# A hybrid encoder block on one Trainium2 core: the residual stream laid out features by tokens from the output projection on, with the second norm's token scale on gate and gated tiles

## The chip, the cores and the metric

The kernel runs on one core of a Trainium2 chip. The metric is the device time of one execution in microseconds. Engines are named as in the profile: PE is TensorE (matmuls), PEld its weight loads, DVE VectorE, ACT ScalarE, POOL GpSimd, SP SyncE, which issues most DMAs.

## What is computed

One layer over 1024 tokens and 1024 features, in fp32:

```
h = rms_norm(x, norm1_g);  z = h @ w_in
conv_out = conformer_conv(a, gate of z);  attn_out = neighbourhood_attention(q, k, v of z)
x = x + concat(conv_out, attn_out) @ w_out
h = rms_norm(x, norm2_g)          # x / sqrt(mean(x*x over features) + eps) * norm2_g
x = x + (silu(h @ w_gate) * (h @ w_up)) @ w_down      # 2816 hidden features
```

The norm's token scale r = 1/sqrt(...) is one number a token. Since h = (x * norm2_g) * r, gate and up products of x * norm2_g can be multiplied by r afterwards, token by token, as long as r is applied before silu.

## The kernel before

**Matmuls.** Every matmul of the projections is made of three: `mac` (L122, L123, L124) multiplies hi x hi, hi x lo and lo x hi parts. `split` (L113 to L118) makes the parts: ScalarE casts the hi part (L114), VectorE or GpSimd subtracts it from the source for the lo part (L118). The stationary operand is 128 x 128, the moving one 128 x 512. The three big products (output projection, gate and up, down projection) each use a scheme of seven products instead of eight, with sums and differences of quadrants. The quadrants are halves of the tokens (x11, x12 first half, x21, x22 second) by halves of the features.

**Order.** It is written out by hand. `weaves(n, s0=..., s1=...)` makes a list of n entries; after each mac of a product, `weave()` runs the next entry. So `s9=N(0)` puts `norm2_out(0)` behind the tenth mac. `plan[k]` is such a list of four for the k-th product of the FFN. The scheduler places instructions on each engine's queue in program order; an engine runs its queue in order and waits at the head for its operands.

**Output projection** (`group` L1112, `proj` L770, `read` L874). Seven products in the order n1, n7, n4, n6, n5, n2, n3; each has four output tiles of four macs, that is 48 matmuls. The left operand's token tile (128 tokens, from attention output `a11`, or convolution and sums in `qop`) is stationary, 512 features of the weights `wB` or `wP` move, and an output tile holds 128 tokens x 512 features. `fill` runs the first tile of n1 in the last steps of attention. Each result is added on VectorE (L865) into `x2[t]`, one tile of 128 tokens x 1024 features for each of eight t, into which the block's input x is loaded or accumulated by DMA.

**Second norm.** Behind n5 and n3, `norm2(t)` (L943) stores x2[t] to DRAM, squares it on ScalarE with a sum over the row, and takes the root. `norm2_out(t)` (L954) makes xn = x2 * r * g on VectorE. Then `turn(t, j)` (L1067), 16 times, transposes four 128 x 128 blocks of xn on TensorE, since the next products contract over features; ScalarE and VectorE take them out of PSUM: for the first token half straight into hi and lo parts `h2` (the operands A11 and A12), and into `xT`. `s_sum` (L1037, and L1033 for S4, part of it on GpSimd) makes the sums S1 to S4, and `s_split` (L118) their parts and those of A22, all by tiles of 128 tokens.

**Gate and up** (`product` L1166, `evac` L1177). The weight parts `t` are stationary, the token operands move, and results are 128 hidden features x 512 tokens. There are 22 blocks i, each with seven products. The first four are run interleaved in this order, and these are the numbers that `plan` and the prediction use: 0 to 7 are m1(0), m1(1), m2(0), m2(1), m1(2), m1(3), m2(2), m2(3); 8 to 17 are m6(0), m6(1), m5(0), m5(1), m7(0), m7(1), m3(0), m3(1), m4(0), m4(1). m6 reads S2, m5 S1, m7 S3, m3 S4, m4 A22. A product is four macs, 12 matmuls. After each, `prep` splits one more weight tile, the lo part on GpSimd. `evac` combines results: u = B - g (L1185), g = B - g (L1193), g = g - D (L1195), g = B - g (L1197), D = D - u (L1201), the silu on ScalarE (L1191, L1202), and silu x up (L1198, L1205). From block 4 on all seven products of one block follow each other (the FFN's steady part).

**Down projection** (`down` L1358). Seven products over `sd`, which comes back from DRAM; again 128 tokens are stationary and 512 features move.

Of the kernel before, what the change touches and what calls it, by code (L numbers as in the profile page):

```python
# [13 lines left out]
P = 128  # L14
# [17 lines left out]
def layout(v):  # L32
# [21 lines left out]
        "x": f["x"],  # L54
        "xt": f["x"].T.reshape(4, 2, P, 2, 512).transpose(3, 0, 2, 1, 4),
# [6 lines left out]
        "g2": f["norm2_g"][None],  # L62
# [12 lines left out]
def build(ctx, tc, a):  # L75
# [622 lines left out]
    def evac_hi(s_):  # L698
        rh, cb = order[s_]
        if rh == 0:  # L700
            if not rowf:
                rowf.extend(G(f"rf{j}").rearrange("p (c b q) -> p c b q", c=2, b=4) for j in range(2))
            for j in range(2):
                act.copy(rowf[j][:, :, cb], os_[s_][:, 2 * j:2 * j + 2])
        else:
            a11[cb] = [w.rearrange("p (c q) -> p c q", c=4) for w in lr(G(f"a11{cb}", F32R))]
            act.copy(a11[cb][0], os_[s_])

    def evac_lo(s_, js=(0, 1)):
        rh, cb = order[s_]  # L710
        if rh == 0:
            return
        if not diff:
            diff.extend(G(f"df{j}").rearrange("p (c b q) -> p c b q", c=2, b=4) for j in range(2))
        for j in js:
            cs = slice(2 * j, 2 * j + 2)
            hi, lo = [w[:, cs] for w in a11[cb]]
            dve.tensor_tensor(lo, os_[s_][:, cs], hi.bitcast(F32), OP.subtract)
            dve.tensor_tensor(diff[j][:, :, cb], os_[s_][:, cs], rowf[j][:, :, cb], OP.subtract)
# [38 lines left out]
    x2, xn, qop = {}, {}, {}  # L758
# [9 lines left out]
    CB = (0, 3, 1, 2)  # L768
# [83 lines left out]
    def rows(ap, t):  # L852
        rh, cb = divmod(t, 4)
        return ap.rearrange("(h i w) d -> h i w d", h=2, w=GW)[rh, :, cb * 16:cb * 16 + 16, :]

    def load_x2(t):
        x2[t] = G(f"x2{t}")
        nc.sync.dma_start(x2[t], rows(a["x"], t))

    def add_x(t):  # L860
        return lambda: pool.dma_start(x2[t], rows(a["x"], t), accum_op=OP.add)
# [7 lines left out]
    def fill(*cs):  # L869
        if 0 not in pb:  # L870
            pb[0] = mm("n10")
        proj("n1", 0, pb[0], cs)

    def read(p, cb):  # L874
        acc = pb[cb]
        if p == "n1":
            x2[4 + cb] = G(f"x2{4 + cb}")
            l, r = lr(x2[4 + cb])
            act.copy(l, acc)
            dve.tensor_scalar(r, acc, -1.0, None, op0=OP.mult)  # L880
        elif p == "n7":
            put(cb, 1, acc, OP.subtract)
            put(cb, 0, acc)
        elif p in ("n4", "n6"):
            put(cb, 0, acc, OP.add if p == "n4" else OP.subtract)
        elif p == "n5":
            put(cb, 1, acc)
            put(4 + cb, 1, acc)
            norm2(cb)
        elif p == "n2":  # L890
            put(4 + cb, 0, acc)
        else:
            put(4 + cb, 1, acc)
            norm2(4 + cb)
# [3 lines left out]
    for i in range(2, 32 + 2):  # L898
# [32 lines left out]
        if i > 2:  # L931
# [3 lines left out]
            elif i > 6 and i % 4 in (0, 3):  # L935
                evac_lo((i + 1) // 4 - 2, (0,) if i % 4 == 3 else (1,))
        if jobs:
# [3 lines left out]
    sd2 = {}  # L941
# [8 lines left out]
    def norm2_out(t):  # L950
        r = SM(f"r2{t}r", 1)
        dve.reciprocal(r, sd2[t])
        xn[t] = G(f"xn{t}")
        dve.scalar_tensor_tensor(xn[t], x2[t], r, g2b, OP.mult, OP.mult)  # L954
# [66 lines left out]
    sn, sop, xT = {}, {}, {}  # L1021

    def s_sum(t, ns, eng):
        (x11, x12), (x21, x22) = lr(xT[t]), lr(xT[t + 4])
        for n in ns:
            if n == 1:
                sn[t] = G(f"sn{t}")
            s1, s2 = lr(sn[t])
            if n == 4:
                if not s4:  # L1030
                    s4.extend(G(f"s4{j}").rearrange("p (k s) -> p k s", s=512) for j in range(2))
                for j in range(2):
                    eng.tensor_tensor(s4[j][:, :, t * P:(t + 1) * P], *[w[:, j * 256:(j + 1) * 256].rearrange(  # L1033
                        "p (k s) -> p k s", s=P) for w in (x12, s2)], OP.subtract)
                continue
            o, l, r = ((s1, x21, x22), (s2, x11, s1), (x21, x11, x21))[n - 1]
            eng.tensor_tensor(o, l, r, OP.subtract)  # L1037

    s4 = []

    def s_rows(n, t):
        return {"S1": lambda: sn[t][:, :512], "S2": lambda: sn[t][:, 512:], "S3": lambda: xT[t + 4][:, :512],
                "A22": lambda: xT[t + 4][:, 512:]}[n]()

    def s_split(n, t, eng=dve):
        if n == "S4":
# [354 lines left out]
```

## Time and profile before

| | |
|---|---|
| runs (3) | 1050.26, 1050.57, 1051.03 us |
| profiled execution | 1050.14 us, of which the span from first to last instruction is 1048.4 us |
| granted TensorE clock, mean | 0.999 |
| busy: PE, PEld, DVE, ACT, POOL | 1028.2, 833.8, 722.9, 465.3, 452.6 us |
| HBM read, written | 122.86 MB, 53.15 MB |

Busy time is the union of an engine's instructions. A group row of the profile names line, engine, operation, output<-input with buffer numbers left out, shapes and count; then total busy time, the mean of one in ns, and the engine's idle time just before them. A row of the timeline is start, duration, engine, line, operation and operands. Projection, attention and convolution fill the span up to about 330 us (n1 begins among them at 317); n2 begins at 380.0 us, product 0 at 406.4.

### The profile page before, as it was taken

The numbers are of one execution on the slowest core, as the hardware profiler recorded it, in microseconds if no ns is written. First come the engines' busy times: TensorE is split into PE (matmuls) and PEld (weight loads), VectorE is DVE, ScalarE is ACT, GpSimd is POOL, SyncE is SP. The second block draws the span as 40 slices with busy tenths as digits, with TensorE's granted clock in tenths as the row PEclk, the third lists the DMA queues.
The fourth block names the chain that finished last, engine by engine and source line by source line (L and its number), as shares of the span: only waits on it lengthen the run. The fifth ranks groups of instructions, "written<-read, shape, count | busy, mean of one in ns | idle before, by whom it ended". The sixth has DMA issues, their size and how long they took to land.

```text
span 1048.4 us, 13903 instructions
## 1 busy us (share of the span) xinstructions
PE 1028.2 (98%) x4972; PEld 833.8 (80%) x4972; DVE 722.9 (69%) x1097; ACT 465.3 (44%) x915; POOL 452.6 (43%) x342
## 2 busy tenths in 40 slices
PE   7999999999999999999999999999999999999997
PEld 5888888776657888778888888888888888888885
DVE  6768998976896575876564655646556567768883
ACT  6466346636776676532232232232322443443441
POOL 0226578833575863655545454455454100002310
PEclk9999999999999999999999999999999999999999
DMA  9496771285536754465232132232232597633641
GB/s 334 178 271 220 225 238 61 77 244 168 148 109 163 159 182 141 109 167 174 104 131 101 71 131 101 89 132 93 99 111 81 207 326 256 205 101 125 215 133 40
DMA packets 74678, 162.93 MB, mean 155 GB/s; under 512 B 13489, under 2 KB 22193, under 8 KB 73905
## 3 DMA queue, kind: packets, MB, share of 16 engines
q1 hardware_dynamic: 67776, 144.14, 40.7%
q0 software_dynamic: 4864, 10.49, 5.9%
q10 hardware_dynamic: 1968, 7.42, 2.0%
q8 instruction: 39, 0.64, 0.2%
q14 instruction: 31, 0.25, 0.1%
HBM read 122.86 MB, written 53.15 MB: 168 GB/s over the span
## 4 chain that ended last, share of the span: by engine, by line
PE 88%; DVE 4%; POOL 2%; DMA 2%; ACT 2%; issue 2%; SPq 0%; POOLq 0%; ACTq 0%; DVEq 0%
PE B L122 5%; PE B L123 5%; PE B L124 5%; PE D L123 4%; PE D L124 4%; PE D L122 4%; PE A L122 3%; PE A L123 3%; PE A L124 3%; PE z L123 3%; PE z L122 3%; PE z L124 3%; PE gl L124 3%; PE gl L123 3%; PE gl L122 3%; PE n L122 3%
## 5 line engine op out<-in xcount | busy, mean ns | idle before, releaser
L347 DVE SCALAR_TENSOR_TENSOR cv<-u,par,cv 128x1009 f32<-128x1009 f32 (+14 forms) x85 | 108.5, 1276 | 2.0
L373 POOL TENSOR_TENSOR pa<-pa,pr 128x1022 f32<-128x1022 f32 (+10 forms) x31 | 75.2, 2426 | 33.7 <-ACT pr L372 32.2
L1356 POOL TENSOR_TENSOR ou<-ou,resm 128x512 f32<-128x512 f32 x8 | 12.5, 1571 | 142.5 <-DMA resm<-xd 142.5
L114 ACT CAST op<-sr 128x512 fp32r<-128x512 f32 x77 | 47.7, 619 | 52.7 <-PE B2d L124 21.3
L118 DVE TENSOR_TENSOR op<-sr,op 128x512 fp32r<-128x512 f32 x77 | 58.2, 756 | 16.4 <-ACT op L114 16.4
L1193 DVE TENSOR_TENSOR g<-B,g 128x512 f32<-128x512 f32 x22 | 15.2, 690 | 71.3 <-PE B L124 68.2
L1202 ACT ACTIVATE D<-D 128x512 f32<-128x512 f32 x22 | 12.8, 582 | 112.5 <-DVE D L1201 112.5
L1185 DVE TENSOR_TENSOR u<-B,g 128x512 f32<-128x512 f32 x22 | 15.2, 691 | 61.0 <-PE B L124 61.0
L668 POOL TENSOR_SCALAR e<-e,rs 128x288 f32<-128x288 f32 (+1 forms) x64 | 35.0, 568 | 45.6 <-DVE rs L666 41.0
L114 ACT CAST op<-wd 128x512 fp32r<-128x512 f32 x66 | 40.9, 620 | 30.4 <-DVE wd L1280 17.4
L118 DVE TENSOR_TENSOR op<-wd,op 128x512 fp32r<-128x512 f32 x66 | 50.5, 765 | 1.9 <-ACT op L114 0.3
L986 DVE TENSOR_TENSOR ts<-ts,gu 128x512 f32<-128x512 f32 x36 | 43.3, 1203 | 0.6
L1191 ACT ACTIVATE A<-A 128x512 f32<-128x512 f32 x18 | 10.5, 582 | 68.6 <-PE A L124 68.6
L661 ACT ACTIVATE e<-e,mx 128x288 f32<-128x288 f32 (+1 forms) x64 | 36.3, 569 | 2.9 <-DVE mx L659 2.8
L659 DVE CUSTOM_DVE_ANT_0 e<-s,tab 128x288 f32<-128x288 f32 (+1 forms) x64 | 29.7, 501 | 8.7 <-PE s L646 8.4
L372 ACT ACTIVATE pr<-u,par 128x1022 f32<-128x1022 f32 (+10 forms) x31 | 34.2, 1135 | 1.2 <-ACT vs L433 1.2
L677 PEld LDWEIGHTS p<-ident,e 128*96 128x96 f32 (+1 forms) x192 | 20.0, 133 | 18.1 <-POOL e L668 10.4
L677 PE MATMUL p<-ident,e 128*96 128x128 f32 (+1 forms) x192 | 28.5, 281 | 2.3 <-DVE pT L682 1.0
L986 DVE TENSOR_TENSOR ts<-gu 128x512 f32<-128x512 f32 x18 | 30.1, 1670 | 0.0
L865 DVE TENSOR_TENSOR x<-x,n 128x512 f32<-128x512 f32 x32 | 21.0, 681 | 13.1 <-PE n L124 13.1
L693 PE MATMUL o<-pT,vw 96*64 96x128 f32 (+1 forms) x384 | 28.0, 281 | 0.0
L646 PE MATMUL s<-kT,qT 64*128 64x288 f32 (+1 forms) x128 | 26.7, 495 | 0.0
(1066 smaller groups left out, 3524.1 us busy)
## 6 DMA issues: line engine op xcount, KB each, us to landing
sr<-sd SPq DMA_DIRECT2D x77, 256.0 KB
gu<-in_gu SPq DMA_DIRECT2D x36, 512.0 KB
sd<-sd SPq DMA_DIRECT2D x22, 512.0 KB
wd<-in_wd SPq DMA_DIRECT2D x44, 256.0 KB
sd<-g SPq DMA_DIRECT2D x33, 256.0 KB
x<-in_x SPq DMA_DIRECT2D x12, 512.0 KB
xd<-x SPq DMA_DIRECT2D x8, 512.0 KB
resm<-xd SPq DMA_DIRECT2D x16, 256.0 KB
```

What stands on the lines that cost most here:

```text
L114: act.copy(hi, src)
L118: eng.tensor_tensor(*[w[..., sl] for w in (lo, src, hi.bitcast(F32))], OP.subtract)
L122: pe.matmul(acc, lh, rh, start=start, stop=False, skip_group_check=True)
L123: pe.matmul(acc, lh, rl, start=False, stop=False, skip_group_check=True)
L124: pe.matmul(acc, ll, rh, start=False, stop=stop, skip_group_check=True)
L347: dve.scalar_tensor_tensor(acc[:, o], uc[:, i], dwk[:, c, t:t + 1], acc[:, o], OP.mult, OP.add)
L372: act.activation(pr[:, o], uc[:, i], AF.Copy, scale=dwk[:, c, t:t + 1])
L373: pool.tensor_tensor(pa[:, o], pa[:, o], pr[:, o], OP.add)
L661: act.activation(e[:, hh], e[:, hh], AF.Exp, bias=mx, scale=-1.0, accum_out=rs[:, hh:hh + 1])
L668: pool.tensor_scalar(es[i][:, hh], es[i][:, hh], rs[:, hh:hh + 1], 1.0, op0=OP.mult, op1=OP.mult)
L677: pe.transpose(pt[:m, g * P:(g + 1) * P], es[i][:, hh, g * m:(g + 1) * m], ident)
L986: dve.tensor_tensor(lr(tsum[i, 1])[n - 3] if o is None else o, l, r, OP.add)
```

## The change

From the output projection on, the weights are stationary and the tokens move, so that each result is 128 features x 512 tokens. Then:

- x2[t] holds, for a token half and a group jb, two tiles of 128 features x 512 tokens. The host hands over x (`x2`) in that layout and lays the output out again; `g2` comes as 128 x 8 numbers into `par`.
- The 16 turns (64 transposes), `norm2`, `norm2_out` and xn are gone. Squares are summed elementwise into one tile for each token half (ScalarE squares, VectorE adds), `token_sums` (TS) sums over the features by four F32 matmuls with a column of ones, VectorE takes the inverse root by small steps (RS; v is its input), and `token_rows` (TR) spreads it over all partitions by four transposes of a broadcast column, copied by ScalarE into `rw` (128 x 1024, a half for each token half).
- Left operands are split with the feature scale g2 in one step (`split2`: ScalarE for hi, a scalar_tensor_tensor on VectorE for lo). The sums S1 to S4 are made in place, all on VectorE, S1 with x22 scaled by ScalarE into PSUM (Y).
- The token scale `rw` is multiplied in `evac`: for the gate tile before silu and for silu x up after it (m2 and m4): four more 128 x 512 operations on VectorE a block.
- n1's first two tiles are cut, since the last window's tokens (columns 256 to 384 of 512) come late: an EARLY part of 256 and 128 columns, and a LATE part of 128.
- Window 0's attention output is parked and its parts split later (`early_split`).
- In the down projection the two operands change places.

The core of the diff:

```diff
-    def lhs(p, c, cb):
+    def right(p, c):
         if p == "n1":
-            return [w[:, c] for w in a11[cb]]
-        q, o = qop[LHS[p]], c * 512 + cb * P
-        return [q[:, o:o + P], q[:, 2048 + o:2048 + o + P]]
+            return [a11[w, c // 2][:, c % 2].rearrange("p b q -> p (b q)") for w in range(2)]
+        return [qop[LHS[p]][:, o + c * 512:o + c * 512 + 512] for o in (0, 2048)]
...
-    def proj(p, cb, acc, cs=range(4), start=True):
+    JB, EARLY, LATE, FULL = range(4), (slice(0, 256), slice(384, 512)), (slice(256, 384),), (slice(0, 512),)
+    def proj(p, jb, acc, cs=range(4), start=True, parts=FULL, woven=True):
         w = wq[RHS[p]]
         for c in cs:
-            mac(acc, lhs(p, c, cb), [w[:, o + c * 512:o + c * 512 + 512] for o in (0, 2048)],
-                start and c == 0, c == 3)
-            weave()
+            for sl in parts:
+                mac(acc[:, sl], [w[:, o + c * 512 + jb * P:o + c * 512 + jb * P + P] for o in (0, 2048)],
+                    [q[:, sl] for q in right(p, c)], start and c == 0 and sl.start == 0, c == 3)
+            if woven:
+                weave()
...
-    def norm2(t):
+    def squares(t):
         nc.sync.dma_start(xd[t * P:(t + 1) * P, :], x2[t])
-        ss = SM(f"s2{t}", 1)
-        act.activation(cv(f"jk{t}"), x2[t], AF.Square, accum_out=ss)
-        sd2[t] = SM(f"r2{t}d", 1)
-        act.activation(sd2[t], ss, AF.Sqrt, bias=eps, scale=1.0 / D)
...
+        act.activation(sq, x2[t], AF.Square)
+        if sqs.get((h, "last")):
+            sqs.pop((h, "last"))()
+        sqs[h, "last"] = lambda: dve.tensor_tensor(sqs[h], sqs[h], sq, OP.add)
+    def sqs_last(h):
+        sqs.pop((h, "last"))()
+        l, r = lr(sqs[h])
+        dve.tensor_tensor(l, l, r, OP.add)
+    def token_sums(h):
+        pt = tp(f"ss{h}")
+        for k in range(4):
+            pe.matmul(pt[:, k:k + 1], sqs[h][:, k * P:(k + 1) * P], one, start=True, stop=True)
+        v, rt[h] = SM(f"v2{h}", 4), SM(f"r2{h}", 4)
+        dve.tensor_scalar(v, pt[:, :4], 1.0 / D, None, op0=OP.mult)
+        rt[h, "steps"] = rsqrt(rt[h], v, f"q2{h}")
+    def token_rows(h):
+        pt = lr(cv(f"rw{h}"))[0]
+        for k in range(4):
+            pe.transpose(pt[:, k * P:(k + 1) * P], rt[h][:, k:k + 1].to_broadcast([P, P]), ident)
+        act.copy(lr(rw)[h], pt)
+    def split2(hi, lo, src, jb, d, eng=dve):
+        g = g2[:, 4 * d + jb:4 * d + jb + 1]
+        act.activation(hi, src, AF.Copy, scale=g)
+        eng.scalar_tensor_tensor(lo, src, g, hi.bitcast(F32), OP.mult, OP.subtract)
...
+        for n in ns:
+            if n == 3:
+                dve.tensor_tensor(x21, x11, x21, OP.subtract)
+            else:
+                o, l, g, r = {1: (y22[jb], x21, ga, y22[jb]), 2: (x11, x11, ga, y22[jb]), 4: (x12, x12, gb, x11)}[n]
+                dve.scalar_tensor_tensor(o, l, g, r, OP.mult, OP.subtract)
...
+    pb[1] = mm("n11")
+    proj("n1", 1, pb[1], parts=EARLY)
+    for jb in range(2):
+        proj("n1", jb, pb[jb], parts=LATE, woven=False)
+        read("n1", jb)
...
-           s7=U(1, 0), s8=U(1, 1), s9=[lo2, lo2, prep], s10=[U(2, 0), take], s11=U(2, 1), s12=[lo2, lo2], s13=prep)
+    weaves(16, s0=take, s2=A(0, 0), s4=A(1, 0), s6=A(2, 0), s8=A(3, 0), s1=lambda: sqs_last(0), s9=[prep, TS(0)], s10=[RS(0), take], s11=[A(0, 1), RS(0)], s12=RS(0), s13=[RS(0), prep], s14=RS(0))
     group("n2")
...
+        9: dict(s0=TS(1), s1=SP("S3", 0), s3=SP("S3", 1)),
+        10: dict(s1=SP("S3", 2), s2=SS(0, 4), s3=RS(1)),
...
+        14: dict(s0=TR(1), s1=SP("A22", 0), s3=SP("A22", 1)),
...
+            dve.tensor_tensor(acc, acc, lr(rw)[0], OP.mult)
             act.activation(sl[i], acc, AF.Silu)
+            scaled.append(lambda: dve.tensor_tensor(sl[i], sl[i], lr(rw)[0], OP.mult))
...
             dve.tensor_tensor(acc, acc, u2[i], OP.subtract)
+            dve.tensor_tensor(acc, acc, lr(rw)[1], OP.mult)
             act.activation(acc, acc, AF.Silu)
             def f():
+                dve.tensor_tensor(r, lr(rw)[1], r, OP.mult)
                 dve.tensor_tensor(r, acc, r, OP.mult)
```

How it moves instructions. On TensorE, in n1's first tile (`n`) at the third contraction step, before; `a` is the attention output, `wB` the weights, the moving operand stands first, and `z` are transposes of the convolution, `o` attention:

```order
L829 MATMUL z_3307<-ident,xh_2202 128x128 x2
L829 MATMUL z_3307<-ident,xh_2358 128x128 x2
L693 MATMUL o_3254<-pT_3280,vw_2742 64x128 x2
L693 MATMUL o_3254<-pT_3280,vw_2745 64x128 x4
L122 MATMUL n_3263<-wB_2699,a_2471 128x512
L123 MATMUL n_3263<-wB_2699,a_2471 128x512
L124 MATMUL n_3263<-wB_2699,a_2471 128x512
```

And the same place now:

```order
L694 MATMUL o_3260<-pT_3249,vw_2743 64x128 x4
L123 MATMUL n_3269<-a_2784,wB_2697 128x256
L124 MATMUL n_3269<-a_2786,wB_2697 128x256
L125 MATMUL n_3269<-a_2784,wB_2697 128x256
L123 MATMUL n_3269<-a_2784,wB_2697 128x128
L124 MATMUL n_3269<-a_2786,wB_2697 128x128
L125 MATMUL n_3269<-a_2784,wB_2697 128x128
```

Three matmuls of 512 columns have become three of 256 and three of 128, and three more of 128 columns follow after attention's end.

On VectorE around products 8 to 10, before; `S` are lo parts of S3 and S4, `s` the sums for S4, `u` and `g` reads of gate and up results (`B`):

```order
L118 TENSOR_TENSOR S_4249<-xT_4014,S_4249 128x4x128
L118 TENSOR_TENSOR S_4249<-xT_4055,S_4249 128x4x128
L1185 TENSOR_TENSOR u_4296<-B_4281,g_4080 128x512
L118 TENSOR_TENSOR S_4249<-xT_4094,S_4249 128x4x128
L1033 TENSOR_TENSOR s_4268<-xT_3865,sn_4145 128x2x128
L1033 TENSOR_TENSOR s_4269<-xT_3865,sn_4145 128x2x128
L1185 TENSOR_TENSOR u_4318<-B_4301,g_4117 128x512
L118 TENSOR_TENSOR S_4249<-xT_4130,S_4249 128x4x128
```

And now; `v` reads the token sums `ss` of the second half, the `q21` are small steps of the inverse root, and `x` holds x2 and the sums made in place:

```order
L1221 TENSOR_TENSOR u_4224<-B_4209,g_4041 128x512
L982 TENSOR_SCALAR v_4238<-ss_4233 128x4
L994 SCALAR_TENSOR_TENSOR S_4244<-x_3409,par,S_4244 128x512
L994 SCALAR_TENSOR_TENSOR S_4244<-x_3424,par,S_4244 128x512
L1221 TENSOR_TENSOR u_4255<-B_4229,g_4065 128x512
L994 SCALAR_TENSOR_TENSOR S_4244<-x_3452,par,S_4244 128x512
L1080 SCALAR_TENSOR_TENSOR x_3346<-x_3346,par 128x512
L821 TENSOR_SCALAR q21w<-v_4238 128x4
L822 TENSOR_SCALAR q21g<-q21w 128x4
L823 TENSOR_SCALAR q21g<-q21g 128x4
L1231 TENSOR_TENSOR g_4041<-B_4209,g_4041 128x512
L1229 TENSOR_TENSOR sl_4084<-sl_4084,rw 128x512
```

Two splits of S3 stood ahead of the first u; now all four stand behind v, which waits for TensorE's token sums, with the sums for S4, the small steps and the scaling of sl among them.

More of the change, by code (lines that the diff above doesn't have):

```diff
@@ L699, in evac_hi, with early_split @@
         rh, cb = order[s_]
[L700 to L707, printed above, removed]
+        if rh == 0 and not rowf:
+            rowf.extend(G(f"rf{j}").rearrange("p (c b q) -> p c b q", c=2, b=4) for j in range(2))
+        if s_ == 1:
+            early.append(ST("early").rearrange("p (c q) -> p c q", c=4))
+            act.copy(early[0], os_[s_])
+            return
+        if rh == 1 and not a11:
+            a11.update({(w, j): G(f"a11{w}{j}", F32R).rearrange("p (c b q) -> p c b q", c=2, b=4)
+                        for w in range(2) for j in range(2)})
+        for j in range(2):
+            act.copy((a11[0, j] if rh else rowf[j])[:, :, cb], os_[s_][:, 2 * j:2 * j + 2])
+    early = []
+    def early_split(j):
+        hi, lo = [a11[w, j][:, :, 0] for w in range(2)]
+        split(hi, lo, early[0][:, 2 * j:2 * j + 2], (dve,))
     def evac_lo(s_, js=(0, 1)):
@@ L1080, in build @@
-    g2b = G("g2b")
-    nc.sync.dma_start(g2b, a["g2"].to_broadcast([P, D]))
+        split2(*[q[:, 4 * d + jb] for q in h2], lr(x2[jb])[d], jb, d)
     skip = lambda: None
@@ L1197, in evac @@
             dve.tensor_tensor(l, acc, l, OP.subtract)
+            while scaled:
+                scaled.pop(0)()
             dve.tensor_tensor(l, sl[i], l, OP.mult)
```

231 lines of the change are left out of this document (111 added, 120 removed).

## The prediction

> **What bounds the kernel now.** I read the page first: the span, the busy table, the chain that ended last.
>
> ```profile
> span 1048.4 us, 13903 instructions
> PE 1028.2 (98%) x4972; PEld 833.8 (80%) x4972; DVE 722.9 (69%) x1097; ACT 465.3 (44%) x915; POOL 452.6 (43%) x342
> PE 88%; DVE 4%; POOL 2%; DMA 2%; ACT 2%; issue 2%; SPq 0%; POOLq 0%; ACTq 0%; DVEq 0%
> ```
>
> TensorE is busy for 98% of the span, so a microsecond of its instructions that goes is a microsecond gained, unless something else makes it wait. VectorE is busy 69% on average, and what it has free lies unevenly. So I read the busy time by stretch: n2 and n3; products 0 to 15 of the FFN; and a piece of its steady part.
>
> ```profile
> 380.30:406.30 26.00, 26.00 (x136) 21.67 (x135) 17.56 (x27) 18.67 (x36) 9.88 (x6) 1.00 0.55 181
> 406.30:456.10 49.80, 47.64 (x219) 38.21 (x217) 41.79 (x48) 29.65 (x55) 27.84 (x22) 1.00 0.40 116
> 600.00:770.00 170.00, 170.00 (x752) 140.77 (x751) 96.46 (x118) 49.06 (x90) 83.44 (x63) 1.00 0.29 106
> ```
>
> The columns are length, then busy time and count of PE, PEld, DVE, ACT and POOL, then granted clock, DMA share and GB/s. Only the middle stretch has TensorE idle: 49.80 - 47.64 = 2.16 us. There VectorE is busy 84% of the time. The waits of TensorE between 330 and 460 us say on whom:
>
> ```profile
> PE B L122 <- DVE u L1185: 1.4, 1, 1.4
> PE D L123 <- DVE A L118: 0.4, 1, 0.4
> PE B L123 <- DVE S L118: 0.3, 1, 0.3
> ```
>
> All three are on VectorE, whose queue is full there. The change puts other work into just this queue.
>
> **The change part by part: TensorE.** The first two rows are the starts of two matmuls of 512 columns that lie twelve apart; the next two are the starts of two blocks of four transposes with three matmuls between them; the last counts all transposes.
>
> ```profile
> 420.04 0.39 PE L122 MATMUL A<-h,t2m 128*128 128x512 f32 x1
> 422.76 0.39 PE L122 MATMUL A<-h,t3m 128*128 128x512 f32 x1
> ...
> 407.06 0.60 PE L1067 MATMUL t<-ident,xn 128*128 128x128 f32 x4
> 408.20 0.60 PE L1067 MATMUL t<-ident,xn 128*128 128x128 f32 x4
> ...
> L1067 PE MATMUL t<-ident,xn 128*128 128x128 f32 x64 | 9.6, 272 | 0.0
> ```
>
> 2.72 us / 12 = 0.227 us a matmul. One block of four transposes and three matmuls takes 1.14 us, so four transposes take 1.14 - 3 x 0.227 = 0.46 us, 0.115 each. The 64 transposes go: 16 x 0.46 = 7.36 us removed. I also take the stretch's 2.16 us of waits off, and work out the new waits afresh below.
>
> TensorE gets three things. First, eight transposes of the broadcast token scale: 2 x 0.46 = 0.92. Second, eight F32 matmuls of one column for the token sums. In the trace an F32 matmul leaves two records: the scores are 64 instructions in the code, and this row counts
>
> ```profile
> L646 PEld LDWEIGHTS s<-kT,qT 64*128 64x128 f32 x128 | 9.6, 184 | 6.0 <-issue 5.9 <-DVE mx L659 0.2
> ```
>
> 128. So 16 passes; with a 128-column weight load each, I price them like the transposes, 16 x 0.115 = 1.84 (0.92 a half). No one-column matmul is in the trace; by one pass each it would be 0.9, by a 512-column matmul for each pass 3.6. Third, 24 matmuls of n1 (two feature blocks, four contractions, three products) are cut in pieces: 24 of 256 columns and 48 of 128, for 24 x 0.227 = 5.45 us before. At half of 0.227, about 0.12, and the transposes' 0.115: 24 x 0.12 + 48 x 0.115 = 8.4, so +2.95. The trace has no matmul of hi and lo parts below 512 columns: by columns alone the pieces would cost nothing more (+0); if a 128-column piece took as long as a 512-column one, 24 x 0.12 + 48 x 0.227 = 13.8, +8.3. I take 2.95 because the transposes have the same tile and column count. [...]
>
> Elsewhere stationary and moving operands only change places, at equal shapes and counts: 0.
>
> TensorE alone, then: -7.36 - 2.16 + 0.92 + 1.84 + 2.95 = **-3.8 us**.
>
> **The change part by part: VectorE between n5 and product 17.** Norm scaling, splits and sums of the FFN's left operands are issued here as before, but as operations on whole 512-column tiles, and with new ones among them. What one costs is in the groups between 330 and 480 us. All of these read two operands from SBUF:
>
> ```profile
> L118 DVE TENSOR_TENSOR S<-s,S 128x512 fp32r<-128x512 f32 x4 | 8.3, 2108 | 0.0
> L118 DVE TENSOR_TENSOR S<-sn,S 128x512 fp32r<-128x512 f32 x8 | 6.6, 858 | 4.9 <-ACT S L114 4.8
> L118 DVE TENSOR_TENSOR S<-xT,S 128x512 fp32r<-128x512 f32 x4 | 4.0, 1013 | 2.7 <-ACT S L114 2.7
> L1037 DVE TENSOR_TENSOR sn<-xT 128x512 f32<-128x512 f32 x4 | 3.8, 958 | 1.1 <-ACT xT L1078 1.1
> L1037 DVE TENSOR_TENSOR xT<-xT,xT 128x512 f32<-128x512 f32 x4 | 3.8, 1002 | 0.0
> L1037 DVE TENSOR_TENSOR sn<-xT,sn 128x512 f32<-128x512 f32 x4 | 3.7, 935 | 0.1
> L118 DVE TENSOR_TENSOR A<-xT,A 128x512 fp32r<-128x512 f32 x4 | 3.1, 804 | 0.0
> ```
>
> 32 operations, 33.3 us: 1.04 each, and since a record runs some 0.07 us into the next start (0.67 against 0.60 in the rows below), I take 1.0 in a full queue. One operand from PSUM is cheaper, and steady:
>
> ```profile
> L1185 DVE TENSOR_TENSOR u<-B,g 128x512 f32<-128x512 f32 x4 | 2.7, 684 | 3.5 <-PE B L124 3.5
> 451.89 0.67 DVE L1195 TENSOR_TENSOR g<-g,D 128x512 f32<-128x512 f32 x1
> 452.49 1.18 DVE L118 TENSOR_TENSOR A<-xT,A 128x512 fp32r<-128x512 f32 x1
> ```
>
> From one start to the next, 0.6. The first kind varies because of GpSimd. One split of S4 took 4.54 us while GpSimd's splits of the weights ran without a break:
>
> ```profile
> 442.92 1.74 POOL L118 TENSOR_TENSOR t1m<-gum,t1m 128x512 fp32r<-128x512 f32 x1
> 444.18 1.73 POOL L118 TENSOR_TENSOR t0m<-gum,t0m 128x512 fp32r<-128x512 f32 x1
> 445.42 1.73 POOL L118 TENSOR_TENSOR t1m<-gum,t1m 128x512 fp32r<-128x512 f32 x1
> ...
> 443.16 4.54 DVE L118 TENSOR_TENSOR S<-s,S 128x512 fp32r<-128x512 f32 x1
> ```
>
> GpSimd's weight splits stay, one a product. The small steps of the inverse root and one wide operation are priced by
>
> ```profile
> L818 DVE SCALAR_TENSOR_TENSOR rcg<-rcq,rcg 128x8 f32<-128x8 f32 x3 | 0.5, 167 | 0.1
> L954 DVE SCALAR_TENSOR_TENSOR xn<-x,r21r,g2b 128x1024 f32<-128x1024 f32 x1 | 1.3, 1283 | 0.0
> L954 DVE SCALAR_TENSOR_TENSOR xn<-x,r23r,g2b 128x1024 f32<-128x1024 f32 x1 | 2.0, 2043 | 0.0
> ```
>
> 0.17 us, and 1.3 to 2.0 (I take 1.5) for 1024 columns.
>
> All times below count from n5's end. *First place, the scale rows of the first half* (TR(0), three steps into n3). TensorE gets there after n2 (48 x 0.227 = 10.9), the token sums (0.92) and nine matmuls (2.04): 13.8. VectorE must by then have done, in this order: two reads of n5 (1.2), two square sums of 1024 columns (3.0), l + r (1.0), five splits of the first left operands (5.0), three reads of n2 (1.8), v and 13 small steps (14 x 0.17 = 2.4): 14.4. So a wait of 0.6 (0 with splits at 0.7; 1.6 with both sums at 2.0).
>
> *Second place, products 9 to 17.* The second half's token sums stand after the first step of product 9. TensorE is there at 2 x 10.9 + 0.92 + 0.46 + 9 x 2.72 + 0.68 = 48.3 and has them at 49.2. v, which reads them, stands on VectorE ahead of all splits of S3, so that queue goes on at about 49.5 however early it was done. From v to the last split of S4 it holds 14 operations on two SBUF operands (four splits of S3, four sums for S4, four splits of S4, two sl times scale), four with PSUM (2.4) and 13 small ones (2.2): 49.5 + 4.6 + 14 = 68.1. TensorE wants that split at the last step of product 14, at 23.2 + 0.92 + 14 x 2.72 + 2.04 = 64.2. Behind it stand seven more and two with PSUM to the last split of A22: 68.1 + 7 + 1.2 = 76.3; product 16's last step wants it at 64.2 + 2 x 2.72 + 0.46 = 70.1. The wait in all is the larger lateness, 6.2 us. With c for the price of one operation on two SBUF operands, it is 21 x c less 14.8 (70.1 less 49.5 + 4.6 + 1.2): nothing at c = 0.70, 3.1 at 0.85, 10.4 at 1.2.
>
> ScalarE gets four scaled copies and squares as before, at 44% busy on average: 0, covered by what it has free; if that cover went, the scaled copy before a split would come on top of VectorE's lateness, some 0.6 us.
>
> **FFN.** Each of 22 blocks gets four more 512-column operations on VectorE. In this steady stretch it is busy 96.46 of 170 us; 19.05 us a block (84 x 0.227), so 10.8 + 4 x 0.65 = 13.4 busy. The tightest read is g less D before the next product takes D's bank:
>
> ```profile
> 692.95 0.68 DVE L1195 TENSOR_TENSOR g<-g,D 128x512 f32<-128x512 f32 x1
> 695.39 0.39 PE L122 MATMUL D<-A,t14m 128*128 128x512 f32 x1
> ```
>
> It ends 1.76 us ahead; at most one new operation (0.6) can stand before it: 0. Without that slack it would be 22 x 0.6 = 13 us. Loads, stores and the tail keep their order and sizes: 0.
>
> **The sum.** -3.8 + 0.6 + 6.2 = +3.0 us. The profiled execution took 1050.14 us (1.7 more than its span); the median of the runs shown, 1050.57, is 0.43 above it. So 1053.1 profiled and **1053.6** by the median. Its own range, with c from 0.95 to 1.2, is 1052.4 to 1058.2.
>
> **The rivals.**
> - *VectorE keeps up.* If c is near the PSUM row's 0.68, both waits vanish: 1050.57 - 3.8 = **1046.8**. From c = 0.78 down the waits (1.6 + 0.2) leave a gain of 2 us. For it: S<-sn and A<-xT lie at 0.80 to 0.86, and GpSimd's two sums for S4 go to VectorE, so GpSimd holds less. Against it: the 32 rows' mean. [...]
> - *Half of the wait.* At c = 0.85, 3.1 + 0.3 of waits: 1050.57 - 3.8 + 3.4 = **1050.2**, no change that can be told.
> - *Narrow pieces are dear.* If 128 columns of a hi/lo matmul take the 0.227 of 512, n1 costs 48 x (0.227 - 0.115) = 5.4 more: **1059.0**, slower with VectorE late. Nothing speaks for it but that no such matmul is in the trace. From a piece price of about 0.14 on, it takes another microsecond.
>
> **How the numbers follow.** About 0.2%, 2.1 us, is what a measurement of this kernel can tell from no change. Chances: forecast 0.38, VectorE keeps up 0.30, half of the wait 0.20, dear pieces 0.12. The wait's price per c is what divides the first three, and the 32 rows lie nearer to 1.0. Range 1046.0 to 1058.3: rival one with 0.8 to spare, up to the forecast's own end; dear pieces are left out. Faster 0.30, same 0.22 (half of the wait, and a little of the forecast), slower 0.48.
>
> **What would show it.** After: no transposes but eight of rw; a wait of TensorE on r of under 1 us in n3; waits of 3 to 4 us on splits of S4 in product 14 and of about 2 more on A22 in product 16; n1's pieces 0.23 us for each pair of a 256 and a 128; two-SBUF operations on VectorE at 1.0 between. Wrong if TensorE waits nowhere in products 8 to 17, if the pieces start 0.2 apart, or if an FFN block takes more than 19.1 us.

## The result, and the profile after

The changed kernel takes 1059.71 us (median of 5 runs, 1058.87 to 1060.72), the kernel before 1050.26 us beside it. The ratio is 1.0091, 95% interval 1.0076 to 1.0106: slower by 9.4 us, where 3.0 us were forecast, and outside the range given (1046.0 to 1058.3). The profiled execution took 1060.57 us.

The page of after, span and busy times:

```profile
span 1058.9 us, 13987 instructions
PE 1033.4 (98%) x4980; PEld 838.8 (79%) x4980; DVE 779.6 (74%) x1206; ACT 457.0 (43%) x891; POOL 450.8 (43%) x338
```

To see where the time went, I compare the same instructions in both traces. In these rows of the views by tile stand count, the shortest, median and longest in ns, then the first and the last start. `n<-wP,Q` (after: `n<-Q,wP`) opens with n7 and closes with n5, FFN block 4 reaches m6 with `B<-S,t4m`, and `A0d` is the down projection. Before:

```profile
L122 PE MATMUL n<-wP,Q x48: 389/389/481, 333.6 to 379.3; 128*128 128x512 f32 x48
L122 PE MATMUL B<-S,t4m x12: 389/389/389, 491.4 to 504.3; 128*128 128x512 f32 x12
L122 PE MATMUL A0d<-op x44: 389/389/389, 831.4 to 1036.4; 128*128 128x512 f32 x44
```

And after:

```profile
L123 PE MATMUL n<-Q,wP x48: 389/389/481, 336.2 to 382.0; 128*128 128x512 f32 x48
L123 PE MATMUL B<-S,t4m x12: 389/389/389, 504.8 to 517.7; 128*128 128x512 f32 x12
L123 PE MATMUL A0d<-op x44: 389/389/389, 844.8 to 1049.8; 128*128 128x512 f32 x44
```

n7 begins 2.6 us later and n5 ends 2.7 later: that is n1. Block 4 comes 13.4 later, so n2 to product 27 cost 10.7. From there to the last matmul of the down projection nothing is added (13.4). But the span ends only 10.5 later: the tail has become 2.9 us shorter. In a piece of the FFN's steady part TensorE is busy throughout, as before, though VectorE now is for 115.40 of 170 us (before 96.46):

```profile
600.00:770.00 170.00, 170.00 (x751) 140.76 (x750) 115.40 (x152) 49.04 (x90) 86.84 (x63) 1.00 0.29 103
```

So the loss lies between n2 and product 17. TensorE's waits there, in after (us in total, times, longest):

```profile
PE rw L988 <- DVE r L830: 3.3, 1, 3.3
PE D L124 <- DVE A L994: 3.1, 1, 3.1
PE D L124 <- DVE S L994: 2.8, 1, 2.8
PE ss L980 <- DVE sq L975: 0.9, 1, 0.9
```

10.1 us, all on VectorE, where 6.8 were forecast. And behind each of the three long waits the matmuls are slow. The timeline of TensorE at the wait on r, and where each slow stretch ends (start, duration; in brackets the idle time before):

```profile
397.37 0.39 PE L125 MATMUL n<-Q,wB 128*128 128x512 f32 x1
401.02 0.62 PE L988 MATMUL rw<-ident,r 128*128 128x128 f32 x4 [3.26 <-DVE r L830]
...
404.94 0.63 PE L124 MATMUL n<-Q,wB 128*128 128x512 f32 x1
405.37 0.62 PE L125 MATMUL n<-Q,wB 128*128 128x512 f32 x1
405.80 0.43 PE L123 MATMUL n<-Q,wB 128*128 128x512 f32 x1
...
456.78 0.52 PE L125 MATMUL D<-S,t1m 128*128 128x512 f32 x1
...
473.81 0.54 PE L125 MATMUL D<-A,t1m 128*128 128x512 f32 x1
```

Slow matmuls start 0.43 us apart instead of 0.227, and the granted clock is 0.50 there (402.43 to 405.84, 450.22 to 457.05 and 467.29 to 474.11 us). Eight in n3 (1.6 us lost) and some 13.5 behind each of the other waits (2.7 each): 7.0 us in this execution.

What held VectorE up stands in its own timeline (l + r, two splits, and one of the small steps on 128 x 4 numbers):

```profile
387.62 2.72 DVE L975 TENSOR_TENSOR sq<-sq 128x512 f32<-128x512 f32 x1
391.52 3.98 DVE L994 SCALAR_TENSOR_TENSOR h<-x,par,h 128x512 fp32r<-128x512 f32 x2
444.00 4.75 DVE L821 TENSOR_SCALAR q21w<-v 128x4 f32<-128x4 f32 x1
```

and in GpSimd's at the same moment as the last:

```profile
444.50 1.74 POOL L119 TENSOR_TENSOR t1m<-gum,t1m 128x512 fp32r<-128x512 f32 x1
445.75 1.73 POOL L119 TENSOR_TENSOR t0m<-gum,t0m 128x512 fp32r<-128x512 f32 x1
447.00 1.72 POOL L119 TENSOR_TENSOR t1m<-gum,t1m 128x512 fp32r<-128x512 f32 x1
```

The small step needs 0.17 us elsewhere. Here it began 0.5 us ahead of three weight splits of GpSimd and ended with the third. At its start GpSimd was issuing a DMA (443.71 to 444.91 us). That is not what holds it up: in the run below with VectorE's subtractions GpSimd issues three such DMAs in the same stretch, and no operation of VectorE beside them takes longer than usual (0.15 to 0.17 us for the small steps, 0.68 to 0.75 for 512 columns).

The theory from this: VectorE is late because it stands still while GpSimd subtracts, and the half clock comes of the waits. The rivals: VectorE's order alone makes the waits (r behind the splits, v behind the token sums); the clock is a cost of its own; n1's pieces or the tail are more than they seem.

### The profile page after: what moved, and what is told of

Its sections match the earlier page's. It is cut to its first block, busy times and chain, and to the rows that moved or that the text cites. A ratio compares the mean times of both kernels' runs of the same rounds, so it can differ in the third digit from the quotient of the medians.

```text
span 1058.9 us, 13987 instructions
## 1 busy us (share of the span) xinstructions
PE 1033.4 (98%) x4980; PEld 838.8 (79%) x4980; DVE 779.6 (74%) x1206; ACT 457.0 (43%) x891; POOL 450.8 (43%) x338
## 4 chain that ended last, share of the span: by engine, by line
PE 85%; DVE 7%; ACT 3%; DMA 2%; issue 2%; POOL 1%; SPq 0%; POOLq 0%; ACTq 0%; DVEq 0%
PE B L123 5%; PE B L124 5%; PE B L125 5%; PE D L124 4%; PE D L125 4%; PE D L123 4%; PE A L123 3%; PE A L124 3%; PE A L125 3%; PE z L124 3%; PE z L123 3%; PE z L125 3%; PE gl L125 3%; PE gl L123 3%; PE gl L124 3%; PE n L123 2%
## 5 line engine op out<-in xcount | busy, mean ns | idle before, releaser
L1399 POOL TENSOR_TENSOR ou<-ou,resm 128x512 f32<-128x512 f32 x8 | 13.5, 1695 | 139.3 <-DMA resm<-xd 139.3
L1228 ACT ACTIVATE A<-A 128x512 f32<-128x512 f32 x18 | 10.5, 582 | 72.0 <-DVE A L1227 72.0
L1227 DVE TENSOR_TENSOR A<-A,rw 128x512 f32<-128x512 f32 x22 | 15.4, 698 | 26.5 <-PE A L125 26.5
L678 PEld LDWEIGHTS p<-ident,e 128*96 128x96 f32 (+1 forms) x192 | 19.9, 133 | 18.4 <-POOL e L669 10.7
```

What stands on the lines that cost most here:

```text
L678: pe.transpose(pt[:m, g * P:(g + 1) * P], es[i][:, hh, g * m:(g + 1) * m], ident)
```

## The experiments

Medians beside the runs of the kernel before on the same chip (1050.25 to 1050.44 us); brackets hold the 95% interval of the ratio.

**GpSimd's subtractions left out.**

```diff
+        if stage[0] and sub == (pool,):
+            act.copy(lo, src)
+            return
...
-            split(*top[i, p], src, (pool,))
+            if stage[0]:
+                hi = top[i, p][0]
+                act.copy(hi, src)
+                top[i, p] = hi, hi
+            else:
+                split(*top[i, p], src, (pool,))
```

The first part stands in `split` and is for n3's weights, the second in `prep` for the FFN's; `stage[0]` is set from n2 to product 17. The kernel leaves out the true lo parts there, so its output is another.

> The changed kernel without GpSimd's subtractions for weight lo parts from n2 to product 17 (the lo part of the FFN's weights is the hi part again, that of n3's weights a copy by ScalarE, so the numbers that come out are others; the matmuls are the same). Theory (VectorE is late because GpSimd's bursts hold it up): the waits on VectorE in n2, n3, products 12 and 16 vanish, 10.1 us, and with them the half-speed stretches, 7.0 us: about 1042.6 us (1042 to 1046). Rival (the order of VectorE's queue alone makes the waits: r behind the splits, v behind the token sums): more than half of the waits stay, 1050 us or more.

1042.91 us, ratio 0.9929 [0.9914, 0.9943]. The clock is 1.0 throughout, and the longest wait between n2 and product 17 is 0.3 us; all of them together are 0.7 us instead of 10.1:

```profile
PE rw L993 <- DVE r L835: 0.3, 1, 0.3
```

The whole loss hangs on GpSimd's subtractions, and under it lies a gain of 7.5 us (2.9 of them the tail's). It is also what the first rival forecast (1046.8) less the tail's 2.9, within 1 us.

**The same subtractions by VectorE.**

```diff
+        if stage[0] and sub == (pool,):
+            sub = (dve,)
```

This stands in `split`, from n2 to product 17.

> The changed kernel with the weight lo parts of n2 to product 17 subtracted by VectorE instead of GpSimd, at the same places of the program. Theory (while GpSimd subtracts, VectorE's operations on two SBUF operands stand still, so a GpSimd subtraction of 1.25 to 1.7 us costs VectorE about that much): doing it itself costs VectorE 0.6 us, so it gains 0.65 us or more on each of some 22 subtractions, up to 14 us, and the lateness of 8.6 us goes: waits of 2 us or less in all, no half speed, 1042.9 to 1046 us. Rival (VectorE's queue is simply too long, and GpSimd takes work off it): 13 us more in a full queue, 1065 us or more.

1054.77 us, ratio 1.0042 [1.0025, 1.0059]: 4.9 us faster than the changed kernel, with 24 more operations in VectorE's queue between n2 and product 17. The rival is out by 10 us. The groups of VectorE between 384 and 470 us, first after, then this run:

```profile
L119 DVE TENSOR_TENSOR S<-x,S 128x512 fp32r<-128x512 f32 x8 | 7.0, 907 | 1.0 <-ACT S L115 1.0
L994 DVE SCALAR_TENSOR_TENSOR A<-x,par,A 128x512 fp32r<-128x512 f32 x4 | 6.1, 1565 | 0.0
L821 DVE TENSOR_SCALAR q21w<-v 128x4 f32<-128x4 f32 x1 | 4.7, 4749 | 0.0
L1227 DVE TENSOR_TENSOR A<-A,rw 128x512 f32<-128x512 f32 x4 | 2.8, 692 | 0.0
```

```profile
L123 DVE TENSOR_TENSOR S<-x,S 128x512 fp32r<-128x512 f32 x8 | 5.3, 686 | 0.0
L998 DVE SCALAR_TENSOR_TENSOR A<-x,par,A 128x512 fp32r<-128x512 f32 x4 | 2.8, 746 | 0.0
L825 DVE TENSOR_SCALAR q21w<-v 128x4 f32<-128x4 f32 x1 | 0.2, 165 | 0.0
L123 DVE TENSOR_TENSOR t0m<-gum,t0m 128x512 fp32r<-128x512 f32 x5 | 3.4, 686 | 1.2 <-ACT t0m L117 1.2
```

`A<-A,rw` has its first operand in PSUM, and took 0.69 even in after. With no subtraction of GpSimd beside them, the operations on two SBUF operands of 512 columns take 0.68 to 0.75 us in the mean of every group, the added splits too. The theory's time, 1042.9 to 1046 us, was not reached, though: it is out by 8.8 us. One stretch of half speed (3.4 us) and 7.4 us of waits are left:

```profile
PE rw L992 <- DVE r L834: 2.6, 2, 1.7
PE B L127 <- DVE u L1226: 1.9, 1, 1.9
PE D L128 <- DVE A L998: 1.0, 1, 1.0
PE A L127 <- ACT g L1223: 1.0, 1, 1.0
PE ss L984 <- DVE sq L979: 0.9, 1, 0.9
```

The splits now stand in VectorE's queue right behind ScalarE's cast that they read, and the queue stops for it (1.2 us ahead of one of the five in the group above, several times in all).

**TensorE kept busy in its waits.**

```diff
+    def busy(l, r, n, name):
+        def f():
+            w = cv(name)[:, :512]
+            for _ in range(n):
+                pe.matmul(w, l(), r(), start=True, stop=True, skip_group_check=True)
+        return f
...
+        16: dict(s1=busy(lambda: sop["A22"][0][0][:, :P], lambda: sop["A22"][0][0], 22, "b2")),
```

> The changed kernel with extra matmuls, whose result nobody reads, put on TensorE just ahead of its three long waits: 11 of 512 columns before the scale rows TR(0) in n3, 10 before the last step of product 12, 22 before the third step of product 16. The waits themselves are VectorE's lateness and stay. Theory (the clock follows the waits): with the waits filled the granted clock stays at 1.0; of the 7.0 us that slow matmuls cost in the profile of after, 1.6 behind TR(0) and 2.7 behind A22 are saved, the 2.7 behind S3 only lengthen the wait on A22, since VectorE has no idle time between: 1059.7 - 4.3 = 1055.4 us (1054.0 to 1056.5). Rival (the clock falls for another reason, such as load): the same half-speed stretches, 1059.7 us or more.

1059.68 us, ratio 1.0085 [1.0068, 1.0101]: the same as the changed kernel. Where after had half speed for 3.4, 6.8 and 6.8 us, all three stretches are gone, and the one that this run has (3.4 us) stands behind a wait of 1.8 us on the second half's r that after did not have: the clock does follow the waits. But the 4.3 us are not there: 43 idle matmuls (9.8 us) and 4.8 us of waits have taken the place of waits and slow matmuls. Slow matmuls fell into time in which TensorE would have had to wait for VectorE anyway. So the clock moved the loss to another place; it was not a cost of its own, to within some 2.4 us (the intervals of the two runs, 1.6 and 1.7 us, together). The executions of the changed kernel point the same way: the one with a mean clock of 0.991 took 1060.57 us, those with 0.994 and 0.995 took 1058.87 to 1060.72.

**Another order, two of them.** The first puts the second token sums into product 5, splits two to three products earlier and m6(2), m6(3) ahead of m5(0):

```diff
-        9: dict(s0=TS(1), s1=SP("S3", 0), s3=SP("S3", 1)),
...
+        5: dict(s0=[SS(3, 2), SP("S1", 0)], s1=SP("S2", 1), s2=TS(1), s3=SP("S1", 1)),
...
+        7: dict(s0=RS(1), s1=[SP("S3", 0), RS(1)], s2=RS(1), s3=[SP("S3", 1), RS(1)]),
```

> The changed kernel in another order, same operations: the small steps to r of the first half directly behind the token sums and ahead of two splits, TR(0) five steps later; the second token sums in product 5 instead of 9 and its small steps in 6 and 7; splits of S1, S3, S4 and A22 two to three products earlier; products m6(2) and m6(3) ahead of m5(0), so that S3, S4 and A22 are wanted 5.4 us later. Theory (VectorE has idle time early and is late by 8.6 us in all; its waits make the half-speed stretches): no wait over 1 us, clock 1.0, 1059.7 - 10.1 - 7.0 = 1042.6 us (1042 to 1046). Rival (GpSimd's bursts fill VectorE's time wherever the work stands): waits of 5 us or more stay, 1050 us or more.

1057.12 us, ratio 1.0059 [1.0044, 1.0074]; 2.6 us better than the change. The theory's 1042.6 is wrong, and the rival right. The waits on r and on VectorE's splits of S3 and A22 are gone, but others of the same size stand elsewhere between 330 and 600 us, among them 2.8 us at 483.6 us, in block 3:

```profile
PE D L123 <- DVE g L1248: 3.4, 2, 2.8
PE A L123 <- ACT g L1217: 3.0, 1, 3.0
PE B L123 <- ACT S L115: 1.2, 1, 1.2
PE B L123 <- DVE u L1220: 1.1, 1, 1.1
```

The second keeps the products' order and takes four of GpSimd's splits into n3 instead:

```diff
-    weaves(16, s1=A(1, 1), s2=TR(0), s3=prep, s4=A(2, 1), s7=[A(3, 1), prep])
+    weaves(16, s1=A(1, 1), s3=prep, s4=A(2, 1), s7=[TR(0), A(3, 1), prep], s5=prep, s9=prep, s11=prep, s13=prep)
...
-        prep()
+        if n >= 4:
+            prep()
```

> The changed kernel with the early scale rows of the run above, the second token sums in product 5 and the splits of S1, S3, S4 and A22 two to three products earlier (the order of the products as in the changed kernel), and four of GpSimd's weight splits moved from products 0 to 3 into n3, where VectorE has idle time. Theory (GpSimd's splits cost VectorE their own time, some 1.3 us each, while its queue is full): 4 x 1.3 = 5 us less lateness, and some 3 us by the earlier order; waits of 2 us or less in products 12 to 17, no half speed: 1046 to 1050 us. Rival (order alone, as in the earlier reordering run): 1055 us or more.

1059.36 us, ratio 1.0087 [1.0072, 1.0102]: the theory's 1046 to 1050 is wrong, and the rival right. One wait of 7.1 us on u (a read of m6's result) stands behind splits that now come ahead of it in VectorE's queue. Both runs say the same: with GpSimd's work in the stretch, order moves the wait; it does not remove it.

**The wait on r alone.**

```diff
+    weaves(16, s0=take, s2=A(0, 0), s4=A(1, 0), s1=lambda: sqs_last(0), s9=[prep, TS(0)], s10=[*[RS(0)] * 5, A(2, 0), take], s11=A(3, 0), s12=A(0, 1), s13=prep)
...
-    weaves(16, s1=A(1, 1), s2=TR(0), s3=prep, s4=A(2, 1), s7=[A(3, 1), prep])
+    weaves(16, s1=A(1, 1), s3=prep, s4=A(2, 1), s7=[TR(0), A(3, 1), prep])
```

> The changed kernel with only the first of the four waits treated: the small steps to r of the first half directly behind the token sums and ahead of two splits, TR(0) behind the eighth step of n3 instead of the third. Theory (TensorE's time behind n3 is set by VectorE's lateness, so a wait that goes early comes back later): the wait of 3.3 us and the 1.6 us of half speed behind it go, n3 to product 8 run 4.9 us earlier, but VectorE, which is busy from the third square sum on, moves less, and the waits on S3 and A22 grow by 1 to 3 us: 1056 to 1058 us. Rival (each wait is a cost of its own): 1059.7 - 4.9 = 1054.8 us or less.

1056.74 us, ratio 1.0068 [1.0052, 1.0083]: 3.0 us gained of the 4.9 that the wait and its slow matmuls had cost, within the theory's 1056 to 1058. TensorE comes earlier to product 2 and waits 3.0 us there for a copy of ScalarE that stands behind its squares; these wait for VectorE's square sums, one at a time.

**n1 in two pieces.**

```diff
-    JB, EARLY, LATE, FULL = range(4), (slice(0, 256), slice(384, 512)), (slice(256, 384),), (slice(0, 512),)
+    JB, EARLY, LATE, FULL = range(4), (slice(0, 256),), (slice(256, 512),), (slice(0, 512),)
```

> The changed kernel with n1's first two tiles cut once, in two pieces of 256 columns (the second one late), instead of 256 and 128 early and 128 late: 48 pieces of 256 instead of 24 of 256 and 48 of 128. Theory (128 and 256 columns both cost 0.11 to 0.12, the price of a weight load): 24 x 0.113 = 2.7 us less for TensorE, 1057.0 us, unless work that now comes late fills no gap. Rival (the early pieces filled gaps of attention's end, so the time is the same): 1059.7 us, with TensorE idle for 2 us or more between 315 and 330 us.

1056.65 us, ratio 1.0061 [1.0044, 1.0077]: 3.1 us less, forecast 2.7. Of these the pieces themselves give 2.1: n7 begins at 334.1 us instead of 336.2. In the timeline of after, two early pieces of 256 columns, one of 128, and late ones of 128:

```profile
325.65 0.28 PE L124 MATMUL n<-a,wB 128*128 128x256 f32 x1
325.77 0.28 PE L125 MATMUL n<-a,wB 128*128 128x256 f32 x1
325.89 0.22 PE L123 MATMUL n<-a,wB 128*128 128x128 f32 x1
...
327.54 0.28 PE L123 MATMUL n<-a,wB 128*128 128x128 f32 x1
327.65 0.28 PE L124 MATMUL n<-a,wB 128*128 128x128 f32 x1
327.76 0.28 PE L125 MATMUL n<-a,wB 128*128 128x128 f32 x1
```

0.12 and 0.11 us from one to the next: a piece of 128 columns costs about as much as one of 256, and neither costs the 0.227 of 512.

**The store's shape, in the kernel before.**

```diff
-            rows(a["out"], 4 * tok + t)[:, :, d * 512:(d + 1) * 512], w)
+            a["out"][tok, t][:, d * 512:(d + 1) * 512], w)
```

> The kernel before with one thing of the change: the output tile is stored to a row of 128 consecutive lines per store instead of 8 x 16 lines spread over the token grid, the host puts the rows back. In the profiles the last store takes 6.3 us from VectorE's last add to the end before, 3.4 us after. Theory (the store's shape makes the tail shorter by 2.9 us): 1050.3 - 2.9 = 1047.4 us. Rival (the tail differs for another reason): 1050.3 us.

1047.47 us, ratio 0.9973 [0.9963, 0.9983], as forecast, and faster than both kernels. The last stores are moved faster. The mean busy share of the 16 DMA engines (a digit is tenths) and GB/s in 40 slices, in before from 1037 to 1050 us, then in this run over the same time:

```profile
DMA  0000000372444455355554554545410000000000
GB/s 0 0 0 0 0 0 0 82 57 19 57 158 170 189 183 113 139 189 208 164 126 139 176 164 164 145 158 189 176 63 0 0 0 0 0 0 0 0 0 0
```

```profile
DMA  0000079305950397019800000000000000000000
GB/s 0 0 0 0 0 284 391 133 0 227 391 189 0 145 391 271 0 69 397 334 6 0 0 0 0 0 0 0 0 0 0 0 0 0 0 0 0 0 0 0
```

The bytes are the same (1.05 MB). Before, the four stores overlap at some 160 GB/s and run on; now each is nearly done, at up to 391, before the next begins. Before, the engines are busy for some 0.5 on average while the stores run, now for 0.9 at the peaks, so a store of 8 x 16 lines seems to occupy only some of the engines. Whether that is the reason was not tried.

**Waits of known length, in the kernel before.** Chains of ScalarE copies between two reads of a running result:

```diff
+            act.copy(s[:, 0:1], acc[:, 0:1])
+            for j in range(k):
+                act.copy(s[:, 1 + j % 2:2 + j % 2], s[:, 0:1])
+            act.copy(s[:, 3:4], acc[:, 0:1])
```

> The kernel before with nine waits put into TensorE's stream in the FFN, one in every second block from 5 to 21, each made by a chain of small ScalarE copies (1, 3, 5, 7, 9, 11, 13, 15, 18 of them between two reads of the running result), so about 0.7 to 4.5 us long. Theory (a wait of about 2.8 us or more halves the granted clock for 3.4 or 6.8 us, a shorter one doesn't): half-speed stretches of 3.4 or 6.8 us behind the last four or five waits, none behind the first four. Rival (the clock fell in the changed kernel for another reason): clock 1.0 throughout.

1067.34 us (one run). The waits came out shorter than meant, 0.53 to 2.41 us, and only one was followed by half speed: that of 1.87 us. Those of 2.10 and 2.41 were not. So neither side holds as it was put, and longer waits were needed:

> The kernel before with nine waits of about 2.2 to 4.5 us in its FFN (16 to 36 small ScalarE copies). Theory (the clock is decided in fixed steps of 3.413 us, and halves for the next step where TensorE was idle for more than about 1.8 us of one): every wait of 3.6 us or more halves the clock, those between 2.2 and 3.6 us only where they lie for more than 1.8 us in one step of the grid, and all half-speed stretches start a whole number of 3.413 us apart. Rival (a wait over a fixed length of about 2.8 us does it): each wait over 2.8 us, none below.

1094.00 us (one run). Of the nine waits those of 2.19, 3.08, 3.30, 3.52, 3.97 and 4.42 us halve the clock, those of 2.41, 2.63 and 2.85 don't. Two of them in the timeline, and the windows around (the clock is the third number from the end):

```profile
514.33 0.52 PE L122 MATMUL B<-S,t5m 128*128 128x512 f32 x1 [2.19 <-ACT prb L1302]
638.98 0.50 PE L122 MATMUL B<-S,t11m 128*128 128x512 f32 x1 [2.85 <-ACT prb L1302]
```

```profile
513.00:519.00 6.00, 4.67 (x13) 3.69 (x14) 0.69 (x1) 1.80 (x14) 1.54 (x2) 0.72 0.28 80
636.00:642.00 6.00, 3.15 (x14) 2.53 (x14) 0.69 (x1) 3.25 (x25) 2.54 (x2) 1.00 0.05 8
```

A fixed length is out: 2.19 does it, 2.85 does not. The theory of the grid says for all nine what they do. The step is in after's trace: its record of the granted clock has half speed for 3.413, 6.827 and 6.827 us, and 44.373 and 10.240 us at full clock between them, that is 1, 2, 2, 13 and 3 times 3.413. The slow stretches of this run begin 49, 61, 74, 87 and 101 steps of 3.413 us after the first (by the timeline they end at about 518.1, 685.3, 729.6, 774.1, 818.4 and 862.8 us); those of after end at about 405.8, 457.0 and 474.1, that is 15.0 and 5.0 steps apart; and each lasts 3.41 or 6.83 us. With the timelines of both runs of this kind laid on this grid, every step at full clock in the FFN in which TensorE had no matmul for 1.87 us or more is followed by half speed, and none with 1.84 or less: the wait of 2.85 is cut into 1.43 and 1.43. A slow step that itself has 0.8 us or more without a matmul is followed by another one (three times in this run, twice in after). The border is not sharp in other runs. A step with 1.71 us was followed by half speed in the run with the wait on r alone, one with 1.89 was not in that with n1 in two pieces, and with VectorE's splits one with only 0.95 us was, in which the eight one-column matmuls stand (1.0 us). What exactly is counted is open.

**Splits by VectorE, with n1 in two pieces, and then in a better order.**

> The run above and n1's first two tiles cut in two pieces of 256 columns: both gains add up, 2.7 to 3.0 us less than the run above (1040 to 1043 us by the theory there).

1053.08 us, ratio 1.0025 [1.0015, 1.0034]: 1.7 us less than without the pieces, of 2.7 to 3.0. The waits are the same as there (7.7 us in all against 7.6), and n7 begins 2.0 us earlier (334.6 us against 336.6). So the gains do add up, as far as the intervals can tell; the pieces are worth 2.0 us.

```diff
+            owed.append(lambda: dve.tensor_tensor(lo, src, hi.bitcast(F32), OP.subtract))
...
+    weaves(16, s0=take, s1=lambda: sqs_last(0), s2=A(0, 0), s3=flush, s4=A(1, 0), s6=take, s7=flush, s9=[TS(0), prep], s10=[RS(0)] * 5, s11=A(2, 0), s12=A(3, 0), s13=[A(0, 1), prep])
```

> The run with VectorE's weight splits and n1's two pieces, in a better order: each of VectorE's weight splits one product behind ScalarE's cast that it reads (it stood still 1.17 us for the cast seven times), the two splits of n3's weights behind the square sums, the small steps to r of the first half directly behind the token sums and ahead of three splits, two scaled copies of ScalarE in n3. Theory (what is left of the waits there is order: 2.6 on r, 0.9 on the square sums, 1.0 on a copy of ScalarE, 1.9 on u, and 1.7 us by one stretch of half speed): most of it goes, 1053.1 us - 2.6 - 0.9 - 1.0 - 1.7 = 1046.9 us, up to 1049 if the wait on u grows. Rival (VectorE's queue is full again, so the time comes back in products 8 to 17): 1052 us or more.

1050.31 us, ratio 1.0001 [0.9991, 1.0011]: clock 1.0, no difference from the kernel before, between theory and rival. 7.8 us of waits on VectorE and ScalarE are left, spread over eight places of 1.7 us at most. VectorE is busy for 43.5 of 50 us between 406 and 456 us, so its queue is nearly full. But ahead of the two waits on u, 1.0 and 1.5 us, it stood still itself for 1.07 and 1.92 us, for casts of ScalarE that its splits read. How much a still better order would gain was not tried.

The fastest version that computes the whole layer is therefore the kernel before with the changed store, at 1047.47 us.

## Why the prediction was wrong

**TensorE's terms held.** Forecast -3.8; by the traces about -4.0: the transposes and the old waits as reckoned, n1's pieces +2.6 (forecast 2.95), two blocks of token sums at 0.98 and 0.92 (0.92), two of scale rows at 0.49 and 0.51 (0.46), each taken with the three matmuls behind it, as the transposes were. The rival of dear pieces names a time near the measured one, 1059.0, by a mechanism that is not there: pieces of 128 columns start 0.11 us apart. That it comes so near is luck. The FFN's four added operations a block cost 0, as said.

**The step that failed is VectorE's price.** The places were right in part: r in n3 and A22 in product 16, but S3 in product 12 instead of S4 in product 14, where TensorE did not wait. What was wrong is the price. The 0.17 us for each small step came from rows of another stretch, and the 1.0 for each split in the first place from a mean over this one. Here one small step took 4.75 us and put S3's last split, not S4's, 2.8 us late; two splits took 3.98 and l + r 2.72, where 2.0 and 1.0 were reckoned. In waits and the slow matmuls within VectorE's lateness, the first place cost 5.8 us (3.3 + 0.9 + 1.6) instead of 0.6, the second 11.3 (2.8 + 3.1 + 2 x 2.7) instead of 6.2. The run without GpSimd's subtractions has 0.7 us of waits left and no half speed, and where VectorE does them itself the same small step takes 0.165 us: the excess comes from GpSimd. The mean c was not far off: by their starts, the 21 operations from v to the last split of A22 took 0.88 us each in after. That a mean describes it at all was the mistake: even the step of 0.165 us ended only with GpSimd's third subtraction, at 448.75 us against 448.72.

ScalarE's share, taken as 0, was not quite that either. VectorE stood 1.7 us for ScalarE's cast ahead of S1's last split, so v ran 2.1 us after its token sums were ready (440.04 against 437.97), and not with them. What that cost by itself no run shows.

**The clock was missing from the sum**, and its 7.0 us are in the trace; but the run with filled waits shows that without it about the same time passes, in waits and idle matmuls.

**The tail was taken as 0** because "loads, stores and the tail keep their order and sizes". Their order and sizes, yes; the store's shape changed, and gives 2.9 us.

Together: -4.0 + 5.8 + 11.3 - 2.9 = +10.2 us; the profiled executions differ by 10.4, the medians by 9.4. The direction was right, and the rival "VectorE keeps up" is what happens once GpSimd is silent.

## What to carry to other kernels

Where VectorE's queue is full, look at what GpSimd does on SBUF operands beside VectorE's operations on two SBUF operands, and try that work on VectorE itself. Here a subtraction that GpSimd does in 1.3 to 1.7 us cost more than the 0.6 us that VectorE needs for it: moving 24 of them to VectorE made the kernel 4.9 us faster. Before pricing a chain of small operations on the path, look at what GpSimd does at that very moment. And look at the shape of the last store: here 2.9 us lay in it.

## What the runs showed of the hardware

- Operations of VectorE on two SBUF operands took longer where GpSimd subtracted at the same time: in after l + r took 2.72 us and two splits 3.98, in the run with VectorE's subtractions 0.69, and 0.746 each. A one-operand operation of 128 x 4 numbers took 4.75 us beside three subtractions of GpSimd, and 0.165 with none. Operations with one operand in PSUM kept their time (`A<-A,rw` 0.69 us in both runs).
- The granted clock went to 0.50 behind waits of TensorE, in after for 3.413, 6.827 and 6.827 us, with 44.373 and 10.240 us between: whole multiples of 3.413 us. In the two runs with waits of known length, those of 1.87 and 2.19 us, which lay in one step of this grid, were followed by half speed, and so were the five of 3.08 us and more; those of 2.10, 2.41 (once in each run), 2.63 and 2.85 us, which a grid point cut into parts of 1.6 us at most, were not.
- At full clock matmuls of hi and lo parts start 0.11 us apart with 128 columns, 0.12 with 256 (both n1 in after), 0.227 with 512.
- Four stores of 256 KB ran at some 160 GB/s as 8 x 16 lines, and at up to 391 as 128 lines in a row; the kernel became 2.9 us shorter.
